# Layer-norm statistics of the second half by ScalarE, and a newer eviction as the marker of late input splits

## The chip, the cores and the metric

The kernel runs on one core of a Trainium2 chip. The metric is the device time of one execution in microseconds (us); lower is better. The engines are named as the profile names them: PE (TensorE, matmuls and transposes), DVE (VectorE), ACT (ScalarE), POOL (GpSimd) and SP (SyncE, which here only issues transfers).

## The reference

Two layers over 1024 tokens of width 1024: a gated linear recurrence (HGRN2), then a causal convolution module. Each is followed by a layer norm, a squared-ReLU MLP of width 4096, and another layer norm.

```python
for i in range(DEPTH):                       # DEPTH = 2
    mix = hgrn2_mixer(x, ...) if i % 2 == 0 else conformer_conv_mixer(x, ...)
    x = layer_norm(DEEPNORM_ALPHA * x + mix, ln_mix_g[i], ln_mix_b[i])
    ff = jnp.square(jax.nn.relu(x @ ffn_w1[i])) @ ffn_w2[i]
    x = layer_norm(DEEPNORM_ALPHA * x + ff, ln_ffn_g[i], ln_ffn_b[i])

def layer_norm(x, g, b):
    mu = jnp.mean(x, axis=-1, keepdims=True)
    var = jnp.mean(jnp.square(x - mu), axis=-1, keepdims=True)
    return (x - mu) * lax.rsqrt(var + LN_EPS) * g + b

# the end of hgrn2_mixer: o is (1024, 1024) after the recurrence and its own norm
return (o * silu(g)) @ w_out
```

All is in float32. The change concerns layer 0, where the recurrence's output is multiplied by `w_out` (the output projection), normed, and then multiplied by `ffn_w1[0]`.

## The kernel before

**Products.** A float32 product is made of three passes in the type fp32r. Each operand is split into a high part (a cast by ACT) and a low part (a subtraction by DVE, operand minus high part), and PE adds high times high, high times low and low times high. So an operand is ready for PE only after a cast by ACT and then a subtraction by DVE. The tensor with index 0 in its second dimension is the high part and with index 1 the low part.

**Forms.** The large products save multiplications as Strassen and Winograd do: two operands of 2 x 2 blocks are combined to seven forms each, and seven products take the place of eight. They run in the order `ORDER = (1, 2, 6, 5, 7, 3, 4)`. Forms 1 and 2 multiply single blocks; forms 6, 5 and 7 need sums or differences of blocks on both sides, form 3 on the side of the weights alone and form 4 on the side of x alone.

**The stages around the change.** The tokens fall into two halves of 512, each of four tiles t of 128. The output projection of half 0 comes first, then that of half 1. For each tile two products of 24 matmuls give 128 x 512 each; DVE adds the residual into `y[half][:, t]`, and `x1_block(half, t)` norms the tile and sends a copy to DRAM (`keep`). `norm` takes the statistics on DVE (two `bn_stats`, shown as BATCH_NORM_STATS2, and an aggregation), has POOL raise the variance to the power -1/2 (L518), and applies gain and offset in two DVE steps (SCALAR_TENSOR_TENSOR). `act_norm`, used elsewhere in the kernel, takes the sum and the sum of squares by two ACT passes with an accumulated output (L1083 and L1085 of the program before), writing the passed values into a tile `junk` that nobody reads.

The transposed halves are the blocks of x for the first MLP's up products (`Up`). PE transposes a normed tile against `ident` into a PSUM tile. From half 0 come forms 1 and 2 of x. From half 1 `x1_first(t)` makes form 5 and `x1_second(t)` form 6; they also leave unsplit values of forms 7, 3 and 4 in `late_x`. Those are split later by `x1_late(i, k)`: for i = 7, 3, 4 and each of the two pairs of 128-row blocks (k = 0 and k = 2) one cast of 128 x 1024 by ACT and one subtraction by DVE into `xf[i]`. These six calls are background chores; the first products of the MLP call them one after another. In the profile the tiles `xf[i]` are called x1f, `late_x` is xl (forms 7 and 3) and x (form 4), and all weights in use fw.

**The marker.** Ahead of each split `x1_late` has POOL copy one column into the tile that the split will write (L1191). Its value is overwritten at once; it is a marker, there so that the split is ordered behind whatever its source column depends on. Before, the source is the low part of the next weight in the queue.

**Weights of the first MLP.** `Up.form(c, i, f)` runs two products of 12 matmuls with form i of chunk c (eight chunks of 512 columns). The weights come as raw blocks by DMA. DVE adds blocks for the forms 6, 5, 7 and 3 of the first two chunks into tiles called `sum`, ACT casts them (L72), DVE subtracts (line 204, which is the line of every operation that DVE, PE and POOL's timed helper issue). `Up.form` evicts the PSUM of the opening forms into tiles called c by an ACT copy (L1266), for other forms adds PSUM into such a tile by DVE, and applies ReLU and the square by ACT (L1240 and L1241, `put`). The first products go in this order: forms 1 and 2 of chunk 0, forms 1 and 2 of chunk 1, then forms 6, 5, 7, 3, 4 of chunk 0, and the same of chunk 1.

**Sums in DRAM.** After all forms of chunk 0 the kernel calls `block_sums`, which prepares sums of blocks of the second MLP matrix in DRAM: a small transfer on SP's queue that waits for the last weight's low part (L418), two plain copies on SP's queue (L419, L420), and three transfers that POOL issues and that add to what is in DRAM (L421, L423, L423), each after the landing of the one before.

**What sets the order.** Up to `order.close()` (L1038), ahead of the output projection's second half, the order of instructions is written out by hand. Behind it a scheduler places the instructions of each engine by its own model of when operands are ready. The code's order is only its start, so a change in one dependence can move instructions of any engine. On the chip each engine then works through its list in order. The same holds for the DMA queues: a transfer that waits holds back those behind it on its queue.

**Memory.** The program places tiles by hand in 220 KB a partition with `view(kb, ...)`; a tile that is placed over another waits for the last use of that one.

Of the kernel before, what the change touches and what calls it, by code (L numbers as in the profile page):

```python
# [8 lines left out]
F32 = mybir.dt.float32  # L9
# [11 lines left out]
HT = 512  # L21
# [247 lines left out]
def body(ctx, tc, d, out):  # L269
    nc = tc.nc  # L270
# [9 lines left out]
    def view(kb, shape, dt=F32, name="t"):  # L280
        at, top = int(kb * 1024), KBYTES * 1024
        if at < edge[0]:
            if edge[0] < top:
                space.tile([P, (top - edge[0]) // 4], F32, name="gap")
            edge[0] = 0
        if at > edge[0]:
            space.tile([P, (at - edge[0]) // 4], F32, name="gap")
        edge[0] = at + (prod(shape) + 7) // 8 * 32
        return space.tile([P, *shape], dt, name=name)
# [788 lines left out]
    def act_norm(yt, g, b, junk, behind=None):  # L1078

        if behind is not None:  # L1080
            nc.gpsimd.tensor_copy(out=junk[:, :1], in_=behind)
        m = stat.tile([P, 5], F32, tag="mv", name="mv")
        nc.scalar.activation(junk, yt, AF.Copy, accum_out=m[:, 0:1])  # L1083
        vector.tensor_scalar(out=m[:, 1:2], in0=m[:, 0:1], scalar1=-1.0 / D, scalar2=None, op0=ALU.mult)
        nc.scalar.activation(junk, yt, AF.Square, bias=m[:, 1:2], accum_out=m[:, 2:3])  # L1085
        vector.tensor_scalar(out=m[:, 3:4], in0=m[:, 2:3], scalar1=1.0 / D, scalar2=LN_EPS, op0=ALU.mult, op1=ALU.add)
        power_m_half(m[:, 4:5], m[:, 3:4], 1)
        vector.scalar_tensor_tensor(out=yt, in0=yt, scalar=m[:, 1:2], in1=g, op0=ALU.add, op1=ALU.mult)
        vector.scalar_tensor_tensor(out=yt, in0=yt, scalar=m[:, 4:5], in1=b, op0=ALU.mult, op1=ALU.add)

    def norm(yt, g, b):
        mu, rs = moments(yt)
        vector.scalar_tensor_tensor(out=yt, in0=yt, scalar=mu, in1=g, op0=ALU.subtract, op1=ALU.mult)
        vector.scalar_tensor_tensor(out=yt, in0=yt, scalar=rs, in1=b, op0=ALU.mult, op1=ALU.add)
# [40 lines left out]
    g, b = gain(192, "ln_mix", 0)  # L1135
    y = [view(160 + 16 * h, (NTB, D), F32, "y") for h in range(2)][::-1]
    for half in range(2):
        for t in range(NTB):
            nc.sync.dma_start(out=y[half][:, t], in_=d["x"][half * HT + t * P : half * HT + (t + 1) * P])
    late_x = {4: view(212, (4, HT), F32, "x4")}  # L1140
    early = [Slots(nc, vector, slots((204,), "fw"), raws((0,))), Slots(nc, vector, slots((112, 120), "fw"), raws((96, 100)))]
    early.append(Slots(nc, vector, slots((144,), "fw"), raws((152,))))

    xf = {i: view(kb, (2, 4, HT), F32R, f"x1f{i}") for i, kb in ((6, 0), (5, 16), (3, 32), (1, 64), (2, 80), (7, 96), (4, 128))}
# [43 lines left out]
        less(x4, x4, of(xf[2], t, 1).bitcast(F32))  # L1188

    def x1_late(i, k):  # L1190
        nc.gpsimd.tensor_copy(out=xf[i][:, 0, k, :1], in_=fw.queue[0][:, 1, :1].bitcast(F32))  # L1191
        split(xf[i][:, 0, k : k + 2], xf[i][:, 1, k : k + 2], late_x[i][:, k : k + 2])

    def x1_block(half, t):
        norm(y[half][:, t, :], g, b)
        keep(half, t, y[half][:, t, :])
        if half == 0:
            bg.chores += [lambda k=k: turn(y[0][:, t, :], xf[1 + k // 4], t, k, 4) for k in (0, 4)]
            return
        if t == 0:  # L1200
            bg.done()
            late_x.update({i: view(kb, (4, HT), F32, "xl") for i, kb in ((7, 176), (3, 184))})
        if t < NTB - 1:
            bg.chores += [lambda: x1_first(t), lambda: x1_second(t)]
# [23 lines left out]
    class Up:  # L1228
# [23 lines left out]
        def form(self, c, i, f, copies=None, late=False):  # L1252

            u = self.of.setdefault(c, {})
            opens, turned = (1, 2, 3 if c == self.turned else 5), c == self.turned
            for q in range(2):
                parts = [(two(f, slice((q * 4 + k) * P, (q * 4 + k + 1) * P)), two(self.xf[i], k)) for k in range(4)]
                if i == 1:
                    u["z", q] = self.zs()
                if i in opens[1:]:  # L1260
                    u["w", q] = self.ws()
                ps = u["w" if i in (2, 5, 3) else "z", q]
                product(ps, parts, i in opens)
                if i in (1, 6, opens[2]):
                    t = u[i, q] = (copies or self.c)()
                    nc.scalar.copy(out=t, in_=ps)  # L1266
                elif i == 4:
                    self.put(u["h", q], 1, 0, self.c(), ps, -1.0)
                elif turned and i == 5:
                    t = u[6, q]  # L1270
                    vector.tensor_tensor(out=t, in0=t, in1=ps, op=ALU.add)
                    self.put(u["h", q], 0, 1, t, t, 1.0)
                    u[5, q] = u[3, q]
                    vector.tensor_tensor(out=u[5, q], in0=ps, in1=u[5, q], op=ALU.subtract)
                else:
                    t = u[{2: 1, 7: 5, 3: 6}[i], q]
                    vector.tensor_tensor(out=t, in0=t, in1=ps, op=ALU.add)
                    if i == 2:
                        if not late:
                            self.first(u, q)  # L1280
                        continue
                    m, n, scale = {7: (1, 1, -1.0), 3: (0, 1, 1.0)}[i]
                    self.put(u["h", q], m, n, t, t, scale)
            if i == 4:
                for q in range(2):
                    b = [[u["h", q][:, k, :, n * 256 : (n + 1) * 256] for n in range(2)] for k in range(2)]
                    t = {i: self.t() for i in (5, 6, 7, 4)}
                    forms_of(b, lambda i: t[i])
                    for i, src in ((1, b[0][0]), (2, b[1][0]), (3, b[1][1]), *t.items()):
                        store(self.layer, c, i, q, src)  # L1290
                del self.of[c]
# [164 lines left out]
    fw = Forms(nc, vector, slots((144, 152, 48, 112, 120), "fw"), raws(run(192, 4, 4)), raws(run(160, 2, 4), "sum"), lambda after: spare(after, True), 3, range(44))  # L1456
    fw.todo = [[(blocks("w1q", 0, c), 2 if c < 2 else 0)] for c in range(NFC)]
    up = Up()
# [25 lines left out]
    y = [view(32 + 16 * h, (NTB, D), F32, "y") for h in range(2)]  # L1484
    fw = Slots(nc, vector, slots([112, 120, 144, 152, 128, 136, 168], "dw"), raws([192, 196, 200, 204, 160, 164], "dr"), spare, 6, range(10, 50))
    fh = Slots(nc, vector, slots([0, 8, 16, 24, 96, 104, 176], "dh"))
    g, b = gain(184, "ln_ffn", 0)
# [300 lines left out]
    for op, i in steps:  # L1788
# [25 lines left out]
        elif op == "UB":  # L1814
# [5 lines left out]
            if i == NEAR - 1:  # L1820
# [5 lines left out]
                up = LateUp(xs)  # L1826
# [11 lines left out]
        else:  # L1838
# [4 lines left out]
            for k in LATER if i > NEAR else (3, 6, 5, 7, 4):  # L1843
# [3 lines left out]
                if i == NFC - 1 and k == 6:  # L1847
                    fw = Slots(nc, vector, slots([48, 104, 200, 208, 144, 152, 160], "dw"), raws([40, 176, 180, 44, 140, 136], "dr"))
# [7 lines left out]
    y = [view(kb, (NTB, D), F32, "y") for kb in (88, 112)]  # L1856
    g, b = gain(184, "ln_ffn", 1)
# [102 lines left out]
```

## Time and profile before

| | us |
|---|---|
| median of 3 runs | 2057.19 |
| lowest and highest run | 2056.47 and 2060.54 |
| the profiled execution's own time | 2057.16 |
| its span | 2055.4 |
| PE busy in it | 2023.6 |
| DVE busy | 1488.1 |
| ACT busy | 1094.5 |
| POOL busy | 396.3 |

The granted clock of PE averages 0.999 of full speed. The times in the prediction's rows count from the start of the span. In the timeline a row gives the start, the time from the first start to the last end, the engine, the line, the operation with its output and input, how many in a row (x), and in brackets for how long the engine had been idle and what it waited for last. In a row of the view by windows the columns are the window, its length, the busy time and number of instructions of PE, PE's weight loads, DVE, ACT and POOL, then PE's granted clock, the share of the DMA engines and what they moved in GB/s. The second half of the output projection runs from about 470 to 509 us, the MLP's products on forms 1 and 2 from there to 532, and forms 6, 5, 7, 3, 4 of chunk 0 from 532 on.

### The profile page before, as it was taken

The page shows a single profiled execution, that of the slowest core. Times are in us where ns is not written, and L with a number is a line of the kernel's source. Part 1 is how long each engine was busy: PE and PEld are TensorE (multiplying, and loading weights), DVE is VectorE, ACT ScalarE, POOL GpSimd, SP SyncE. Part 2 cuts the span into 40 slices and gives each one's busy share as a digit, 9 for nine tenths or more (in the row PEclk, how much of TensorE's full clock was granted, in tenths as well). Part 3 has the DMA queues.
Part 4 walks back from the last instruction along what each step waited for, and adds up shares of the span by engine and source line. Part 5 has one row for each costly group of instructions (what it writes and reads, how often), then busy time and mean ns, then how long its engine had stood idle before and what let it go on. Part 6 is the DMA issues. An engine that isn't in the chain of part 4 may idle for free. (4 is left out here: it accounts for less than half of the span.)

```text
span 2055.4 us, 29649 instructions
## 1 busy us (share of the span) xinstructions
PE 2023.6 (98%) x11144; PEld 1669.0 (81%) x11144; DVE 1488.1 (72%) x1978; ACT 1094.5 (53%) x1725; POOL 396.3 (19%) x405
## 2 busy tenths in 40 slices
PE   8999999999999999999999999999999999999998
PEld 7888887888787888888888888888888878888886
DVE  8698888877856675665567897889589666754456
ACT  5456565631655556444443776498615555443343
POOL 0112232111101000000001798089110000100002
PEclk9999999999999999999999999999999999999999
DMA  4778999842679776989998744496759768995542
GB/s 187 221 201 229 265 254 269 248 183 85 192 268 295 281 282 225 394 329 329 338 335 299 298 185 184 180 351 247 276 216 337 231 225 303 391 292 195 195 154 103
DMA packets 183944, 517.55 MB, mean 252 GB/s; under 512 B 17912, under 2 KB 49784, under 8 KB 182776
## 3 DMA queue, kind: packets, MB, share of 16 engines
q1 hardware_dynamic: 168312, 456.93, 61.7%
q0 software_dynamic: 15488, 58.72, 12.2%
q8 instruction: 87, 1.43, 0.3%
q14 instruction: 57, 0.47, 0.1%
HBM read 380.85 MB, written 201.85 MB: 283 GB/s over the span
## 5 line engine op out<-in xcount | busy, mean ns | idle before, releaser
L204 PE MATMUL ps<-dw,dh 128*128 128x512 f32 x2688 | 611.3, 389 | 0.5 <-DVE dh L204 0.5
L204 PEld LDWEIGHTS ps<-dw,dh 128*128 128x128 f32 x2688 | 504.3, 188 | 105.3 <-DVE dh L204 0.9
L204 PE MATMUL ps<-x1f,fw 128*128 128x512 f32 x1344 | 307.5, 390 | 5.2 <-ACT c L1266 2.3
L204 PEld LDWEIGHTS ps<-x1f,fw 128*128 128x128 f32 x1344 | 251.5, 188 | 59.7 <-issue 2.5
L204 PE MATMUL ps<-xf,fs 128*128 128x512 f32 x1008 | 248.6, 397 | 3.6 <-issue 1.7
L204 POOL TENSOR_TENSOR cb<-cb,prod 128x512 f32<-128x512 f32 x168 | 223.2, 1337 | 13.0 <-ACT prod L1591 2.4
L204 PEld LDWEIGHTS ps<-xf,fs 128*128 128x128 f32 x1008 | 184.0, 188 | 42.6 <-issue 1.9
L204 DVE TENSOR_TENSOR dh<-dh 128x1024 fp32r<-128x1024 f32 x112 | 136.5, 1222 | 109.4 <-ACT dh L72 109.3
L204 DVE SCALAR_TENSOR_TENSOR ps<-u,par,ps 128x512 f32<-128x512 f32 x296 | 206.0, 750 | 10.6 <-ACT ps L1603 9.3
L204 PE MATMUL ps<-xa,wa 128*128 128x512 f32 x864 | 203.3, 392 | 0.2
L72 ACT CAST dh<-dh 128x1024 fp32r<-128x1024 f32 x112 | 117.5, 1051 | 143.9 <-DMA dh<-hf 137.7
L72 ACT CAST dw<-dr 128x1024 fp32r<-128x1024 f32 x112 | 117.4, 1054 | 140.9 <-PE ps L204 125.5
L204 DVE TENSOR_TENSOR dw<-dr,dw 128x1024 fp32r<-128x1024 f32 x112 | 136.3, 1223 | 76.6 <-ACT dw L72 75.8
L204 PEld LDWEIGHTS ps<-xa,wa 128*128 128x128 f32 x864 | 160.3, 188 | 33.6 <-DMA wa<-ready 0.6
L1591 ACT ACTIVATE prod<-u,par 128x512 f32<-128x512 f32 x168 | 119.4, 726 | 34.2 <-POOL cb L204 33.5
L518 POOL TENSOR_TENSOR mv<-mv,nhalf 128x1 f32<-128x1 f32 x32 | 42.2, 1321 | 405.1 <-DVE mv L204 394.8
L204 PE MATMUL ps<-w,oT 128*128 128x512 f32 x384 | 89.9, 392 | 1.3 <-ACT oT L932 0.8
L204 PE MATMUL ps<-xb,wa 128*128 128x512 f32 x384 | 91.1, 393 | 0.0
L204 PE MATMUL ps<-vw,xf 128*128 128x512 f32 x336 | 79.9, 400 | 5.6 <-ACT vw L435 5.3
L204 PEld LDWEIGHTS ps<-w,oT 128*128 128x128 f32 x384 | 71.4, 188 | 16.6 <-ACT oT L932 1.2
L204 PEld LDWEIGHTS ps<-xb,wa 128*128 128x128 f32 x384 | 71.1, 188 | 14.3
L204 PEld LDWEIGHTS ps<-vw,xf 128*128 128x128 f32 x336 | 65.0, 194 | 20.1 <-ACT vw L435 5.3
(250 smaller groups left out, 2891.9 us busy)
## 6 DMA issues: line engine op xcount, KB each, us to landing
wa<-ready SPq DMA_DIRECT2D x140, 512.0 KB, 5.0
dh<-hf SPq DMA_DIRECT2D x112, 512.0 KB, 5.3
sum_w<-in_w_dram POOLq DMA_DIRECT2D x40, 1024.0 KB, 10.0
ready<-spare SPq DMA_DIRECT2D x76, 512.0 KB, 5.7
raw<-in_w1q_dram SPq DMA_DIRECT2D x66, 512.0 KB, 4.3
dr<-sum_w SPq DMA_DIRECT2D x64, 512.0 KB, 5.5
hf<-ht SPq DMA_DIRECT2D x112, 256.0 KB, 4.9
dr<-in_w_dram SPq DMA_DIRECT2D x48, 512.0 KB, 5.3
```

The source lines that it names most:

```text
L72: self.nc.scalar.copy(out=slot[:, 0, c], in_=raw[:, c])
L204: return op(*args, **kw)
L518: nc.gpsimd.tensor_tensor(out=dst, in0=src, in1=nhalf[:, :n], op=ALU.pow)
L1591: nc.scalar.activation(tp, u[:, k : k + HT], AF.Copy, scale=tap(j, k))
```

## The change

Two things change. In the second half of the output projection the statistics of the four tiles are taken by `act_norm`, and so by ACT, with a new junk tile of 4 KB at 200 KB. And the marker of `x1_late` copies a column of the newest tile that `Up.form` has evicted PSUM into, which is recorded as `up.mark`, in place of the next weight's low part.

```diff
-    late_x = {4: view(212, (4, HT), F32, "x4")}
+    junk, late_x = view(200, (1024,), F32, "junk"), {4: view(212, (4, HT), F32, "x4")}
...
     def x1_late(i, k):
-        nc.gpsimd.tensor_copy(out=xf[i][:, 0, k, :1], in_=fw.queue[0][:, 1, :1].bitcast(F32))
+        nc.gpsimd.tensor_copy(out=xf[i][:, 0, k, :1], in_=up.mark[:, :1])
         split(xf[i][:, 0, k : k + 2], xf[i][:, 1, k : k + 2], late_x[i][:, k : k + 2])

     def x1_block(half, t):
-        norm(y[half][:, t, :], g, b)
+        if half == 0:
+            norm(y[half][:, t, :], g, b)
+        else:
+            act_norm(y[half][:, t, :], g, b, junk)
         keep(half, t, y[half][:, t, :])
...
                 if i in (1, 6, opens[2]):
-                    t = u[i, q] = (copies or self.c)()
+                    t = u[i, q] = self.mark = (copies or self.c)()
                     nc.scalar.copy(out=t, in_=ps)
```

Lines move by up to three: L1240, L1241 and L1266 of the program before are L1243, L1244 and L1269 of the changed one. The lists below are those of the two programs; they say in which order an engine takes its instructions, not when.

First POOL, from the last power of the second half's norms to the third accumulating transfer. The tiles of x are called x1f with a number: before, 4510 is form 7, 4506 form 3 and 4512 form 4; in the changed program 4512 is form 7, 4508 form 3 and 4514 form 4. Before:

```order
L518 TENSOR_TENSOR mv<-mv,nhalf 128x1 x8
L1191 CAST x1f_4506<-fw 128x1 x2
L1191 CAST x1f_4510<-fw 128x1 x2
L421 DMA sum_w_5415<-in_w_dram 128x2x1024
L1191 CAST x1f_4512<-fw 128x1 x2
L423 DMA sum_w_5415<-sum_w_5415 128x1024 x2
```

The same stretch of POOL in the changed program, with c for an evicted tile:

```order
L518 TENSOR_TENSOR mv<-mv,nhalf 128x1 x8
L1191 CAST x1f_4512<-c_5144 128x1 x2
L1191 CAST x1f_4508<-c_5144 128x1
L421 DMA sum_w_5413<-in_w_dram 128x2x1024
L423 DMA sum_w_5413<-sum_w_5413 128x1024
L1191 CAST x1f_4514<-c 128x1
L423 DMA sum_w_5413<-sum_w_5413 128x1024
L1191 CAST x1f_4508<-c 128x1
L1191 CAST x1f_4514<-c 128x1
```

Before, all six markers stand ahead of both L423. In the changed program one for form 4 stands between them, and one each for forms 3 and 4 behind the second.

Next DVE, where the first sums of weight blocks for the forms 5 and 7 of chunk 0 are made. Before (c_5145 and c_5146 are the evicted tiles of form 1 that take the product on form 2; x1f_4504 is form 6, x1f_4509 form 2):

```order
L204 TENSOR_TENSOR xl<-xl,ps 128x4x128
L204 TENSOR_TENSOR x1f_4504<-y,x1f_4504 128x4x128
L204 TENSOR_TENSOR x_4488<-x_4488,x1f_4509 128x4x128
L204 TENSOR_TENSOR sum<-raw 128x1024
L204 TENSOR_TENSOR fw<-raw,fw 128x1024
L204 TENSOR_TENSOR c_5145<-c_5145,ps 128x512
L204 TENSOR_TENSOR sum<-sum,raw 128x1024
L204 TENSOR_TENSOR raw<-raw 128x1024
L204 TENSOR_TENSOR c_5146<-c_5146,ps 128x512
L204 TENSOR_TENSOR fw<-sum,fw 128x1024 x2
```

The same place of DVE in the changed program (c_5143 and c_5144 are those evicted tiles now, x1f_4506 is form 6):

```order
L204 TENSOR_TENSOR fw<-raw,fw 128x1024
L204 TENSOR_TENSOR xl<-xl,ps 128x4x128
L204 TENSOR_TENSOR c_5143<-c_5143,ps 128x512
L204 TENSOR_TENSOR x1f_4506<-y,x1f_4506 128x4x128
L204 TENSOR_TENSOR c_5144<-c_5144,ps 128x512
L204 TENSOR_TENSOR x1f_4512<-xl,x1f_4512 128x1024
L204 TENSOR_TENSOR sum<-raw 128x1024
L204 TENSOR_TENSOR x1f_4512<-xl,x1f_4512 128x1024
L204 TENSOR_TENSOR x1f_4508<-xl,x1f_4508 128x1024
L204 TENSOR_TENSOR sum<-sum,raw 128x1024
L204 TENSOR_TENSOR raw<-raw 128x1024
L204 TENSOR_TENSOR fw<-sum,fw 128x1024 x2
```

The first `sum` stood ahead of both additions into c; now it stands behind them and behind one low part of form 7 of x, with two more low parts of x ahead of the second `sum`.

Last ACT, at the late splits. Before, with L1045 for a cast of x, L72 for that of a weight and L1266 for an eviction:

```order
L72 CAST fw<-sum 128x1024
L72 CAST fw<-raw 128x1024
L1240 ACTIVATE c_5146<-c_5146 128x512
L1045 CAST x1f_4506<-xl 128x1024 x2
L1045 CAST x1f_4510<-xl 128x1024 x2
L1266 COPY c<-ps 128x512
L72 CAST fw<-sum 128x1024
L1045 CAST x1f_4512<-x_4488 128x1024 x2
```

The same casts in the changed program, from the first half of form 3 on:

```order
L1045 CAST x1f_4508<-xl 128x1024
L1243 ACTIVATE c_5144<-c_5144 128x512
L72 CAST fw<-sum 128x1024
L1244 ACTIVATE hr<-c 128x512
L72 CAST fw<-sum 128x1024
L72 CAST fw<-raw 128x1024
L72 CAST fw<-sum 128x1024
L1269 COPY c<-ps 128x512
L1045 CAST x1f_4514<-x_4490 128x1024
L72 CAST fw<-sum 128x1024
L1269 COPY c<-ps 128x512
L1045 CAST x1f_4508<-xl 128x1024
```

Before, the two casts of each late form stood together. Now the first cast of form 3 stands ahead of the first `sum`'s cast; its second stands behind the first cast of form 4, with weight casts and evictions between them.

## The prediction

> **What bounds the kernel now.** I read first the page's busy shares and the waits of PE, then PE's timeline around the change.
>
> ```profile
> PE 2023.6 (98%) x11144; PEld 1669.0 (81%) x11144; DVE 1488.1 (72%) x1978; ACT 1094.5 (53%) x1725; POOL 396.3 (19%) x405
> PE ps L204 <- ACT c L1266: 2.3, 2, 1.5
> PE ps L204 <- ACT fw L72: 1.5, 1, 1.5
> 524.24 8.21 PE L204 MATMUL ps<-x1f,fw 128*128 128x512 f32 x35
> 532.73 0.70 PE L204 MATMUL ps<-x1f,fw 128*128 128x512 f32 x2 [0.28 <-DVE c L204]
> 534.90 11.56 PE L204 MATMUL ps<-x1f,fw 128*128 128x512 f32 x48 [1.47 <-ACT fw L72]
> 547.94 72.36 PE L204 MATMUL ps<-x1f,fw 128*128 128x512 f32 x318 [1.47 <-ACT c L1266]
> ```
>
> PE is the bound, at 98%, so only what makes PE wait moves the time. From the second half of the output projection to the end of the first MLP's up products PE waits three times, 0.28 + 1.47 + 1.47 = 3.2 us: all between the last product on x forms 1 and 2 (ends 532.45) and the first on forms 3 and 7 (547.94). More than 3.2 us cannot be won here; that is 0.16% of 2057, less than the 0.2% that a measurement of this kernel can tell from no change. The undisturbed rate is 72.36 / 318 = 0.2275 us a matmul.
>
> **The statistics by ScalarE.** The last layer norm already uses `act_norm`, so its price is in the trace, beside the bn_stats path of the second half's first tile:
>
> ```profile
> 475.54 0.69 DVE L204 BATCH_NORM_STATS2 bs<-y 128x6 f32<-128x512 f32 x1
> 478.29 1.28 DVE L204 SCALAR_TENSOR_TENSOR y<-y,mv,ln_mix_b 128x1024 f32<-128x1024 f32 x1 [0.44 <-POOL mv L518]
> 2023.99 1.06 ACT L1083 ACTIVATE junk<-y 128x1024 f32<-128x1024 f32 x1 [4.37 <-DVE y L204]
> 2025.37 1.15 ACT L1085 ACTIVATE junk<-y,mv 128x1024 f32<-128x1024 f32 x1 [0.22 <-DVE mv L204]
> 2028.43 1.28 DVE L204 SCALAR_TENSOR_TENSOR y<-y,mv,ln_ffn_b 128x1024 f32<-128x1024 f32 x1 [0.44 <-POOL mv L518]
> ```
>
> From the start of the statistics to the last step of the norm: 2028.43 - 2023.99 = 4.44 us against 478.29 - 475.54 = 2.75, so a tile is ready 1.7 us later, and ACT works about 2.4 us more a tile. DVE saves two bn_stats and an aggregation a tile, about 1.4 us. I cost this at nothing for PE: the order puts the last tile's transposes 24 + 24 + 17 matmuls and eight transposes behind its last product (PE about 524.5, product done 509), and DVE's rows between them end the norm at about 519.6. The margin is 5 us; were it gone, each tile would cost up to 1.7 us. So PE reaches form 5 at 532.45 as before, with the same number of matmuls and transposes ahead.
>
> **The first form's weights come late.** Form 5 needs the cast of `sum` (three blocks of w1) by ACT. DVE's durations there:
>
> ```profile
> 524.52 0.69 DVE L204 TENSOR_TENSOR y<-x1f,ps 128x512 f32<-128x512 f32 x1 [2.24 <-PE ps L204]
> 529.63 1.22 DVE L204 TENSOR_TENSOR sum<-raw 128x1024 f32<-128x1024 f32 x1
> 530.76 1.22 DVE L204 TENSOR_TENSOR fw<-raw,fw 128x1024 fp32r<-128x1024 f32 x1
> 544.37 1.05 ACT L72 CAST fw<-sum 128x1024 fp32r<-128x1024 f32 x1
> 545.32 1.99 ACT L1045 CAST x1f<-x 128x1024 fp32r<-128x1024 f32 x2
> ```
>
> Row to row a 1024-wide DVE step takes 1.13 us (530.76 - 529.63), one of 512 about half that plus 0.03 (0.6), a 1024-wide cast by ACT 0.95 (545.32 - 544.37). In the changed order both adds into the tiles c_5143 and c_5144 and one low part of x form 7 stand ahead of `sum`. The add into c_5144 waits for the last product on form 2 (532.45, seen by DVE at 532.65). Then 0.6 + 1.13: `sum` starts at 534.4 and ends at 535.6, where it began at 529.63 before. ACT casts it by 537.0, behind a cast of x form 3 that a POOL mark releases at 534.4. PE waits 4.6 us. The next sum stands behind two more low parts (2 x 1.13), ends at 539.0, is cast at 540.05; the low part that PE needs then ends at 541.24. PE goes on at 541.3 with 40 of the 48 matmuls: 541.3 + 40 x 0.2275 = 550.4, 2.5 us behind the 547.94 of before.
>
> **The marks go behind the weight sums on POOL.** This is the large term.
>
> ```profile
> 532.39 0.32 SPq L418 DMA_DIRECT2D sum_w<-fw  x1
> 535.56 0.65 SPq L419 DMA_DIRECT2D sum_w<-in_w_dram  x1
> 536.72 3.68 POOL L1191 CAST x1f<-fw 128x1 fp32r<-128x1 f32 x4 [24.43 <-DVE fw L204]
> 542.03 1.27 POOL L421 DMA_DIRECT2D sum_w<-in_w_dram  x1 [1.63 <-DMA sum_w<-in_w_dram]
> 542.83 1.87 POOL L1191 CAST x1f<-fw 128x1 fp32r<-128x1 f32 x2
> 554.56 0.86 POOL L423 DMA_DIRECT2D sum_w<-sum_w  x1 [9.86 <-DMA sum_w<-in_w_dram]
> 563.02 0.81 POOL L423 DMA_DIRECT2D sum_w<-sum_w  x1 [7.59 <-DMA sum_w<-sum_w]
> ```
>
> POOL issues three accumulating transfers, each waiting on POOL for the landing of the one before. In the trace all six marks (L1191) are through before L423 waits. POOL works in order: the last two marks depended on a weight low part of about 538, yet ran only after L421's 1.63 us of waiting. Now the marks hang on evictions, and the order puts one mark for form 4 behind the first L423, and the last for forms 3 and 4 behind the second. ACT's casts that wait for them stand ahead of the weight cast and the evictions that PE needs next.
>
> Step by step. L418 waits for the low part of a weight that ended at 531.98; that DVE row now ends at 530.4 (525.15 for the first row above, 0.63 later as its transposes are later, then 0.72, 0.72, 0.67 for a cast, 0.6, 0.72, 0.6 and 1.22), 1.6 earlier. So L418 at 530.8; with the trace's own steps L419 + 3.17 = 534.0, L421 + 6.47 = 540.45, first L423 + 12.53 = 553.0, second L423 + 8.46 = 561.45. The first mark behind it is done 0.80 + 0.92 us on, at 554.7; ACT casts form 4 and then the weight (0.95 + 1.05), by 556.8. PE, there after six more matmuls at 551.8, waits 5.0 us, does 16 matmuls, and at 560.4 waits for form 3's second half: mark 561.45 + 0.80 + 0.92 = 563.2, cast + 1.1 = 564.3, low part + 1.25 = 565.55. In the trace this matmul, the 24th behind 547.94, starts at 547.94 + 23 x 0.2275 = 553.17. **Sum: 565.55 - 553.17 = 12.4 us later.** The 2.5 us above are inside it, as PE would wait here anyway, and what follows finds its operands ready. The profiled execution took 2057.16 (span 2055.4, 1.8 around it), the median is 2057.19, so they agree: **2069.5 us**.
>
> What is not certain is how long the transfers take to land. The trace's shortest and longest:
>
> ```profile
> 106.08 1.20 POOL L421 DMA_DIRECT2D sum_w<-in_w_dram  x1 [5.05 <-issue]
> 115.96 0.85 POOL L423 DMA_DIRECT2D sum_w<-sum_w  x1 [8.69 <-DMA sum_w<-in_w_dram]
> 122.80 0.87 POOL L423 DMA_DIRECT2D sum_w<-sum_w  x1 [4.55 <-DMA sum_w<-sum_w]
> 311.32 1.20 POOL L421 DMA_DIRECT2D sum_w<-in_w_dram  x1 [3.63 <-issue]
> 324.12 0.86 POOL L423 DMA_DIRECT2D sum_w<-sum_w  x1 [11.60 <-DMA sum_w<-in_w_dram]
> 634.68 0.85 POOL L423 DMA_DIRECT2D sum_w<-sum_w  x1 [7.50 <-DMA ready<-spare]
> 643.88 0.83 POOL L423 DMA_DIRECT2D sum_w<-sum_w  x1 [7.96 <-DMA hf<-ht]
> ```
>
> From L421 to L423 9.88 to 12.80, between the two L423 6.84 to 9.20; so 4.3 less or 1.0 more than taken, a loss of 8.1 to 13.4 us. I take this stage's own 12.53 and 8.46, since nearly the same loads of w1 run beside them.
>
> The Trainium skill, "DMA: Bandwidth & Descriptors", section "Anatomy of one DMA — SWDGE (gpsimd) path", fits such a transfer with about 2.0 us plus its bytes at 436 GB/s. By it, an estimate, the 1 MB transfer would take 4.4 us and the 0.5 MB one 3.2, the marks would come by 549.5, and only the late weights would be left. The trace disagrees: 12.53 and 8.46 us.
>
> **The rivals.**
> 1. The transfers land so early that no mark is late (L421 to L423 under 4.5 us). For it: the last mark is needed only at about 558. Against it: the trace's least is 9.88. Then only the 2.5 us remain: 2059.7. The skill's fit of the last paragraph gives this.
> 2. Not slower: DVE, relieved of 4 x 1.4 = 5.6 us, gets `sum` cast before PE reaches form 5, and the marks ahead of the transfers. It is decided on DVE at `sum`: if it ends before 531.4, the three waits go, 2057.16 - 3.2 = 2054.0. Against it: in the order, the add that waits for PE at 532.65 is ahead of `sum`.
> 3. PE restarts slowly after its long wait. The one long wait in the trace is at the start:
>
> ```profile
> 0.00:10.00 10.00, 4.74 (x11) 3.47 (x12) 3.28 (x5) 4.90 (x7) 0.80 (x8) 1.00 0.76 251
> 15.00:20.00 5.00, 5.00 (x24) 4.14 (x23) 4.44 (x6) 2.88 (x4) 0.00 (x0) 1.00 1.02 409
> ```
>
> After 5.26 us without work PE (first pair of numbers behind the comma) did 11 matmuls in 4.74 us, 0.43 each against 0.21 in the later row; at 0.2275 they take 2.5, so about 2.2 us are lost, with a granted clock of 1.00 (third from the end) all along. After the last wait here (3.9 + 1.0 us) the same would give 2069.5 + 2.2 = 2071.7; after the earlier ones it is hidden by the marks. For it: two waits of over 4.5 us now. Against it: the start may be slow for other reasons, as operands still arrive there. The Trainium skill, "TensorE: Matmul & The Clock Gate", Part 1, states that an idle window of about 3.4 us halves PE's clock until about as long of work; by that rule rival 3 comes true.
>
> **How the numbers follow.** Forecast (marks late, 2064.5 to 2071): 0.58. Rival 3, 2071.7: 0.22. Rival 1, 2059.7: 0.08. Rival 2, 2054.0: 0.06. A further wait that I have not seen, beyond 2074.5: 0.06. The range of 2063.0 to 2074.5 takes the first two with the bounds of the landings and 1.5 us of error in the walk at either end, and leaves out 0.20. Slower by over 0.2% (above 2061.3): 0.58 + 0.22 + 0.06 = 0.86. Within 0.2%: rival 1 and most of rival 2, 0.12; faster: 0.02.
>
> **What would show it.** In the changed profile: PE waits of 4 to 5 us at about 532 for ACT's cast of `fw`; POOL's L1191 standing behind both L423, whose waits for the landings now hold them; ACT idle for 8 us from about 546 and for 5 or so from 557 with POOL as releaser; two PE waits near 552 and 560. L1083 and L1085 four times between 475 and 513, with no PE wait before 532. It is wrong if the L423 waits are short, or if PE waits ahead of 532, where the norms' 5 us of margin would be mis-sized.

## The result, and the profile after

The changed kernel took 2065.87 us (median of 7 runs, 2062.47 to 2071.37), the kernel before 2058.52 (median of 7, 2056.47 to 2060.94). The ratio is 1.0033, with a 95% interval of 1.0018 to 1.0049: slower by 0.3%, some 7 us. The forecast was 2069.5 in a range of 2063.0 to 2074.5.

First the page of the changed kernel (busy times) and the rows of its view of waits that bear on the stage: what PE waited for between 470 and 700 us (in all, times, longest):

```profile
PE 2028.1 (98%) x11144; PEld 1672.0 (81%) x11144; DVE 1482.5 (72%) x1970; ACT 1101.0 (53%) x1741; POOL 395.4 (19%) x405
PE ps L204 <- ACT fw L72: 6.8, 3, 4.6
PE ps L204 <- DVE x1f L204: 0.8, 1, 0.8
```

The profiled execution of the change took 2068.57, that of before 2057.16. Not all of these 11.4 us are the change's. The output projection starts at 416.30 here and at 411.54 in the profile of before, and up to there the code is the same. In the profiles below that start lies anywhere from 413 to 421. So I measure from the stage's own start: from the first matmul on x1f (509.00 before, 513.33 now) to the end of the 432nd, well behind the late splits. Before, the trace has that end at 613.04, so 104.0 us. Now, from PE's timeline:

```profile
513.33 1.07 PE L204 MATMUL ps<-x1f,fw 128*128 128x512 f32 x4
529.75 7.29 PE L204 MATMUL ps<-x1f,fw 128*128 128x512 f32 x31
541.61 2.08 PE L204 MATMUL ps<-x1f,fw 128*128 128x512 f32 x4 [4.57 <-ACT fw L72]
544.70 13.98 PE L204 MATMUL ps<-x1f,fw 128*128 128x512 f32 x50 [1.01 <-ACT fw L72]
559.85 4.22 PE L204 MATMUL ps<-x1f,fw 128*128 128x512 f32 x17 [1.17 <-ACT fw L72]
564.84 98.44 PE L204 MATMUL ps<-x1f,fw 128*128 128x512 f32 x433 [0.76 <-DVE x1f L204]
```

The last row begins with the 168th matmul, and the 432nd ends at 625.20, which is 111.9 us from the start: +7.9. Up to 537.04 there is no wait, so the norms by ScalarE were hidden. Then come the two kinds of wait that the forecast named: 4.57 us for the first weight's cast, and two near 560 and 564. What stands out is how short the last two are. DVE's timeline shows why the first weight is late:

```profile
537.15 0.69 DVE L204 TENSOR_TENSOR c<-c,ps 128x512 f32<-128x512 f32 x1 [0.47 <-PE ps L204]
537.75 1.22 DVE L204 TENSOR_TENSOR x1f<-xl,x1f 128x1024 fp32r<-128x1024 f32 x1
538.89 1.22 DVE L204 TENSOR_TENSOR sum<-raw 128x1024 f32<-128x1024 f32 x1
```

The first sum is behind an addition that itself waits for PE, and behind a low part of form 7. POOL's timeline, with the markers (L1191) and the accumulating transfers:

```profile
532.29 0.77 POOL L1191 CAST x1f<-c 128x1 fp32r<-128x1 f32 x2 [11.80 <-ACT c L1269]
537.90 1.11 POOL L1191 CAST x1f<-c 128x1 fp32r<-128x1 f32 x1 [4.84 <-DVE c L204]
542.66 1.27 POOL L421 DMA_DIRECT2D sum_w<-in_w_dram  x1 [3.64 <-DMA sum_w<-in_w_dram]
555.74 0.86 POOL L423 DMA_DIRECT2D sum_w<-sum_w  x1 [11.81 <-DMA sum_w<-in_w_dram]
556.29 1.48 POOL L1191 CAST x1f<-c 128x1 fp32r<-128x1 f32 x1
561.44 0.81 POOL L423 DMA_DIRECT2D sum_w<-sum_w  x1 [3.68 <-DMA sum_w<-sum_w]
561.98 0.47 POOL L1191 CAST x1f<-c 128x1 fp32r<-128x1 f32 x1
```

POOL waits 11.81 us for the landing ahead of the first L423 and 3.68 for that ahead of the second, and a marker stands behind each. ACT's timeline shows what they hold:

```profile
550.61 0.59 ACT L1269 COPY c<-ps 128x512 f32<-128x512 f32 x1 [0.34 <-PE ps L204]
557.80 1.05 ACT L1045 CAST x1f<-x 128x1024 fp32r<-128x1024 f32 x1 [6.60 <-POOL x1f L1191]
558.76 1.04 ACT L72 CAST fw<-sum 128x1024 fp32r<-128x1024 f32 x1
562.47 1.05 ACT L1045 CAST x1f<-xl 128x1024 fp32r<-128x1024 f32 x1 [2.20 <-POOL x1f L1191]
```

The tile that the first of these markers reads is evicted by 551.2; the marker runs at 556.29, 5 us later. ACT stands idle for 6.60 us for it, then casts form 4 of x, and only then the weight that PE waits for at 559.85. And the clock, by windows (third figure from the end):

```profile
530.00:539.00 9.00, 7.04 (x31) 5.47 (x30) 8.35 (x13) 6.17 (x9) 1.87 (x3) 1.00 0.17 32
540.00:549.00 9.00, 6.38 (x14) 4.59 (x15) 9.00 (x9) 4.18 (x6) 1.27 (x1) 0.50 1.02 279
550.00:559.00 9.00, 8.68 (x39) 6.86 (x37) 2.57 (x3) 2.06 (x4) 2.03 (x2) 1.00 0.77 228
```

Behind the wait of 4.57 us PE runs at half its clock: 14 matmuls in 6.38 us busy, 0.46 each. So PE came late to the markers by itself. Whether the 7.9 us belong to the markers, to the late weights or to the clock cannot be read from this profile alone, since they overlap.

### The profile page after: what moved, and what is told of

It is laid out like the page before. It is cut to its first block, busy times and chain, and to the rows that moved or that the text cites. A ratio compares the mean times of both kernels' runs of the same rounds, so it can differ in the third digit from the quotient of the medians.

```text
span 2066.8 us, 29668 instructions
## 1 busy us (share of the span) xinstructions
PE 2028.1 (98%) x11144; PEld 1672.0 (81%) x11144; DVE 1482.5 (72%) x1970; ACT 1101.0 (53%) x1741; POOL 395.4 (19%) x405
## 3 DMA queue, kind: packets, MB, share of 16 engines
q0 software_dynamic: 15488, 58.72, 12.4%
## 4 chain that ended last, share of the span: by engine, by line
PE 66%; DMA 17%; DVE 7%; issue 5%; ACT 3%; POOL 2%; SPq 0%; DVEq 0%; POOLq 0%; ACTq 0%
PE ps L204 66%; DMA sum_w<-in_w_dram 7%; DMA raw<-in_w1q_dram 1%; POOL cb L204 1%; DMA dr<-in_w_dram 1%; DMA sum_w<-sum_w 1%; DMA next<-in_w1q_dram 1%; DMA next<-in_w_dram 1%; DMA hf<-ht 1%; DVE spare L204 1%; DMA vr<-in_wv_dram 1%; DVE qk L204 1%; DVE fw L204 1%; ACT spare L1448 1%; DVE y L204 1%
## 5 line engine op out<-in xcount | busy, mean ns | idle before, releaser
L204 DVE SCALAR_TENSOR_TENSOR ps<-u,par,ps 128x512 f32<-128x512 f32 x296 | 206.2, 750 | 10.9 <-ACT ps L1606 9.4
L72 ACT CAST dh<-dh 128x1024 fp32r<-128x1024 f32 x112 | 117.4, 1051 | 155.7 <-DMA dh<-hf 155.4
L72 ACT CAST dw<-dr 128x1024 fp32r<-128x1024 f32 x112 | 117.2, 1052 | 128.5 <-PE ps L204 108.9
L1243 ACT ACTIVATE c<-c 128x512 f32<-128x512 f32 x72 | 44.8, 628 | 70.4 <-DVE c L204 70.0
```

The costliest lines, as they stand in the source:

```text
L72: self.nc.scalar.copy(out=slot[:, 0, c], in_=raw[:, c])
L204: return op(*args, **kw)
L1243: nc.scalar.activation(t, src, AF.Relu, scale=scale)
```

## The experiments

Theory M, the forecast's: the markers behind POOL's transfers set the end, and the late weights lie inside. Theory A: the late weights and the half clock behind the long wait set it, and the markers are covered. All results first; "first 432" is the measure above, "waits" PE's waits in it, "half clock" the time in it at a granted clock of 0.50. "Stage" runs from the same start to the first matmul on dw and dh, where the next products begin; the expectations for norm_alone, mark_alone, sums_later and fill_later go by this one. The other expectations quote the first 432 as read from merged rows, within 0.2 us of the table. Each ratio is to runs of before beside it on the same chip, whose medians were 2058.1 to 2060.5.

| kernel | median us | ratio to before (95%) | first 432 | waits | half clock | stage |
|---|---|---|---|---|---|---|
| before | 2058.52 |  | 104.0 | 3.2 | none | 313.2 |
| before_again | 2057.48 (1 run) |  | 104.0 | 3.2 | none | 313.1 |
| the change | 2065.87 | 1.0033 (1.0018 to 1.0049) | 111.9 | 7.5 | 10.2 | 321.1 |
| after_again | 2069.80 | 1.0037 (1.0024 to 1.0050) | 110.7 | 6.5 | 10.2 | 319.6 |
| norm_alone | 2059.04 | 0.9991 (0.9979 to 1.0002) | 106.0 | 3.0 | 6.8 | 312.9 |
| mark_alone | 2064.55 | 1.0023 (1.0008 to 1.0039) | 110.2 | 5.8 | 6.8 | 318.4 |
| sums_later | 2071.89 | 1.0057 (1.0038 to 1.0076) | 109.7 | 5.6 | 10.2 | 324.1 |
| fill_later | 2068.07 | 1.0037 (1.0022 to 1.0053) | 108.5 | 1.9 | 3.4 | 320.7 |
| mark_act | 2063.22 | 1.0022 (1.0012 to 1.0032) | 107.8 | 4.7 | 6.8 | 317.8 |
| last_bn_markact | 2059.05 | 1.0005 (0.9990 to 1.0020) | 105.2 | 3.0 | 3.4 | 312.7 |
| last_bn_old | 2057.97 | 0.9995 (0.9983 to 1.0008) | 104.2 | 3.4 | none | 314.3 |
| bn_markact | 2061.89 | 0.9999 (0.9990 to 1.0009) | 106.3 | 3.4 | 6.8 | 313.7 |
| norm_fill | 2059.32 | 1.0012 (0.9997 to 1.0027) | 104.6 | 0.5 | none | 312.5 |
| mark_act_fill | 2064.62 | 1.0027 (1.0011 to 1.0042) | 107.2 | 2.3 | none | 316.6 |

The two measures can differ, since PE waits again between 655 and 676 us, for 1.9 us before, not at all in norm_alone and 2.8 in mark_act. Differences of the first 432 under 0.4 us say nothing: in the kernels that norm the third tile by ScalarE four more transposes fall into that stretch.

### Each edit alone

norm_alone takes the marker back to the weight's low part; mark_alone takes the norms back.

```diff
 norm_alone:
-        nc.gpsimd.tensor_copy(out=xf[i][:, 0, k, :1], in_=up.mark[:, :1])
+        nc.gpsimd.tensor_copy(out=xf[i][:, 0, k, :1], in_=fw.queue[0][:, 1, :1].bitcast(F32))
 mark_alone:
-        if half == 0:
-            norm(y[half][:, t, :], g, b)
-        else:
-            act_norm(y[half][:, t, :], g, b, junk)
+        norm(y[half][:, t, :], g, b)
```

> The statistics by ScalarE alone; the marker copies the next weight's low part again, as before. Measure: from the first matmul on x1f to the first on dw,dh, 313.18 us before and 321.11 with the change (+7.93). On POOL all six markers stand ahead of both L423. On DVE the first sum stays behind both additions into c, but the low part of form 7 of x no longer stands ahead of it. Theory A (PE waits for late weights, and runs at half its clock behind a long wait): the wait for the first sum's cast is about 4.57 - 1.13 = 3.4 us, one more of 0.5, less the 3.2 us of before, and some 2 us of half clock: +2.7, and the clock shows under 0.9 after the wait. Theory B (the clock has no part): +0.7. Theory C (all of the loss hangs on the markers behind L423): 0 or less.

> The newer marker alone; statistics by bn_stats for all tiles, as before. On DVE the first sum stands ahead of the additions into c again; on POOL one marker of form 3 stands behind the first L423 and one of form 4 behind the second, and PE's list now has twelve matmuls of form 3 in a row, whose second half needs that marker. Measure as above. Theory A, markers behind L423: L418 at 23.4 us from the first matmul on x1f, L421 at 33.0, first L423 at 45.6 to 46.1, low part of form 3 at 49.4; PE is there at 38.8 and waits 10.6 us, then runs at half clock for 3 to 4 us: +11 (9 to 13). Without any part of the clock: +9. Theory C', only late weights matter and markers are covered: -1.5 to +0.5.

norm_alone came to +2.0 in the first 432, with one PE wait:

```profile
544.41 286.39 PE L204 MATMUL ps<-x1f,fw 128*128 128x512 f32 x1248 [2.99 <-ACT fw L72]
```

That is close to A's +2.7, with the half clock behind the wait. But the expectation named the whole stage, and there norm_alone is at -0.3, as C had it: no PE wait of later chunks is left, where before had two more (0.85 and 1.08 us), and the whole kernel is no slower than before. mark_alone came to +6.2 in the first 432 and +5.2 over the stage, less than the +11 that I expected with the markers behind L423, and far from C'. Its POOL, and PE at the markers:

```profile
549.60 0.75 POOL L1191 CAST x1f<-c 128x1 fp32r<-128x1 f32 x1 [2.39 <-ACT c L1266]
558.22 0.86 POOL L423 DMA_DIRECT2D sum_w<-sum_w  x1 [7.87 <-DMA sum_w<-in_w_dram]
558.77 0.51 POOL L1191 CAST x1f<-c 128x1 fp32r<-128x1 f32 x1
```

```profile
541.09 18.23 PE L204 MATMUL ps<-x1f,fw 128*128 128x512 f32 x66 [0.41 <-DVE c L204]
560.41 0.50 PE L204 MATMUL ps<-x1f,fw 128*128 128x512 f32 x1 [1.08 <-ACT x1f L1045]
```

L423 was where I put it (558.22 - 512.30 = 45.9 us from the start; 45.6 to 46.1 expected). But PE needed the second half of form 3 later than I had read from the list: it did 66 matmuls without it, some of them at half the clock. Most of the loss sits with the marker edit: +6.2 against +2.0 in the first 432, +5.2 against -0.3 over the stage.

### The markers taken off POOL's queue

sums_later calls `block_sums` after chunk 1 in place of chunk 0; mark_act leaves it and copies the marker on ACT; bn_markact does the same to mark_alone.

```diff
 sums_later:
-        if c in (0, 2):
+        if c in (1, 2):
             block_sums(*to_sum.pop(0), f[:2, 1, :1].bitcast(F32))
 mark_act, and bn_markact with norm() for all tiles:
-        nc.gpsimd.tensor_copy(out=xf[i][:, 0, k, :1], in_=up.mark[:, :1])
+        nc.scalar.copy(out=xf[i][:, 0, k, :1], in_=up.mark[:, :1])
```

> The change, but block_sums is called after chunk 1 in place of chunk 0, so all six markers stand ahead of L421 on POOL; DVE's list around the first sum is that of the change. Theory A (late weights and the half clock behind them set the end, the markers' wait lies inside it): waits of 4.57 + 1.01 stay, 3.2 of before go, and about 3.7 us are lost at half clock: +6. Theory M (the markers set the end, as forecast; the late weights by themselves are worth 2.5 us): +2.4. Waits near L1191 must be gone in both.

> The change, with the markers copied by ACT in place of POOL, so that no marker stands behind an accumulating transfer and the sums in DRAM stay where they were; DVE's first sum stays behind the additions into c. Measure: the first 432 matmuls on x1f, which took 104.0 us before, 111.8 with the change, 109.7 in sums_later. Theory A (the late weights and the half clock behind the long wait are worth about 5.7, the markers some 2 on top): 109.5, with a PE wait of 4.5 us, half clock behind it, and no wait for L1045 or x1f near the 150th matmul. Theory M (the markers set the end): 106.4.

> mark_alone with the markers copied by ACT: bn_stats for all tiles, the newer marker, no marker on POOL. If the queue behind L423 is what mark_alone pays for (the first 432 matmuls took 110.3 us): 105.0, as last_bn_markact, so -5.3; the wait at the first sums stays at 1.3 to 2.6. If the marker's newer source costs by itself, by the order it makes on ACT and DVE: 109 or more.

sums_later's first 432 were +5.7, close to A's +6; over the stage, which the expectation named, it is +10.9, which neither theory had. Its waits:

```profile
539.06 2.08 PE L204 MATMUL ps<-x1f,fw 128*128 128x512 f32 x4 [4.57 <-ACT fw L72]
542.14 78.29 PE L204 MATMUL ps<-x1f,fw 128*128 128x512 f32 x332 [1.01 <-ACT fw L72]
625.31 89.45 PE L204 MATMUL ps<-x1f,fw 128*128 128x512 f32 x384 [4.87 <-ACT c L1269]
```

The first two are the change's own, and those at the markers are gone. The whole is slower than the change, by a wait that no kernel with the sums in their old place has (4.87 us; 2.61 in fill_later, which moves the sums too). I did not follow it up. It begins at 620.4, where the first 432 have just ended, so it spoils the stage and the whole time but not the first 432. Markers aside, the traces of sums_later and of the change show the same order of work on PE, and for the first 100 us of the stage on DVE and ACT. So sums_later tells what the wait of the markers alone is worth: 109.7 against 111.9 and 110.7, or 1.0 to 2.2 us, as much as PE's last waits in the change's two profiles (1.9 and 1.0).

mark_act came to 107.8, between A's 109.5 and M's 106.4. Its PE still waits 4.25 us for the late weight, and no more for markers:

```profile
538.82 2.08 PE L204 MATMUL ps<-x1f,fw 128*128 128x512 f32 x4 [4.25 <-ACT fw L72]
541.10 2.07 PE L204 MATMUL ps<-x1f,fw 128*128 128x512 f32 x4 [0.20 <-ACT fw L72]
543.38 118.80 PE L204 MATMUL ps<-x1f,fw 128*128 128x512 f32 x520 [0.20 <-DVE fw L204]
```

Against the mean of the change's two profiles, 111.3, that is -3.5 us with the late weights kept. But this edit moves more than the markers: on DVE a late split of x goes behind the second sum, so that the second weight is waited for 0.20 us in place of 1.01, and the half clock lasts 6.8 us in place of 10.2. bn_markact against mark_alone gives 110.2 - 106.3 = 3.9 without the late norms (5.3 expected), again with a sum and an activation in other places; its 106.3 lies between the 105.0 and the 109 that were expected. So waiting behind L423 is worth 1.0 to 2.2 us by itself, and 3.5 to 3.9 with the order that comes with a marker on ACT. Neither theory was right alone, and A was the nearer on what the markers are worth.

### What makes the weights late

```diff
 last_bn_markact (mark_act's marker) and last_bn_old (the marker of before):
-        if half == 0:
+        if half == 0 or t == NTB - 1:
             norm(y[half][:, t, :], g, b)
```

> As mark_act, with the last tile's statistics by bn_stats again (three tiles by ScalarE). In the lists this alone brings the first sum back ahead of the additions into c, but two casts of form 7 of x stand ahead of the first sum's cast on ACT. If the last tile's longer norm is what made the weights late: the PE wait at the first sum falls from 4.57 to 2.0 or less, the first 432 matmuls take 107.6 with a half clock behind that wait (6.8 us of it in mark_alone, whose wait was 2.61) and 105.5 without. If the weights are late for another reason: 109.5, as mark_act.

> Three tiles' statistics by ScalarE, the last by bn_stats, the marker as before. DVE's and ACT's lists at the first sums are nearly those of before. If the statistics by ScalarE are free wherever the last tile is left out: 104.0 within 0.7 for the first 432 matmuls, no PE wait over 1.5 us, no half clock, time as before. If ACT's extra 2.4 us a tile cost PE something of their own: over 105.5.

With bn_stats for the last tile alone, the first sum goes ahead of the addition again (DVE of last_bn_markact), and the long PE wait splits into two short ones:

```profile
530.36 1.22 DVE L204 TENSOR_TENSOR sum<-raw 128x1024 f32<-128x1024 f32 x1
531.50 1.22 DVE L204 TENSOR_TENSOR fw<-raw,fw 128x1024 fp32r<-128x1024 f32 x1
532.63 0.68 DVE L204 TENSOR_TENSOR c<-c,ps 128x512 f32<-128x512 f32 x1
```

```profile
535.63 1.19 PE L204 MATMUL ps<-x1f,fw 128*128 128x512 f32 x4 [1.29 <-ACT fw L72]
538.50 125.75 PE L204 MATMUL ps<-x1f,fw 128*128 128x512 f32 x546 [1.68 <-DVE c L204]
```

From mark_act's 107.8 this is -2.6 us, to 105.2 (105.5 was expected without a half clock, 107.6 with one; 3.4 us of it came). That is the price of the last tile's longer norm with the newer marker; with the old marker it is 1.8 (norm_alone against last_bn_old). PE pays it by the order on DVE. last_bn_old came out at 104.2 and 0.9995, as expected: ACT's statistics for the other three tiles are free, and win nothing. It had one wait over the expected 1.5 (2.11 us at 551.83).

### What the half clock costs

The fill kernels put matmuls that nobody reads into the place of PE's long wait: 20 in fill_later (on sums_later), 13 in norm_fill (on norm_alone), 18 in mark_act_fill (on mark_act).

```diff
+    for _ in range(18):
+        tensor.matmul(banks[:, 3], xf[6][:, 1, 3, :P], xf[6][:, 1, 3], start=True, stop=True)
     up.settle(0)
     fw.ahead(3)
```

> As sums_later, with twenty more matmuls (128x512, high by low part of form 6 of x, into a PSUM bank that nobody reads) between form 2 of chunk 1 and the first form behind it, so that PE is busy while it would have waited 4.57 us. DVE's list is that of sums_later. If the wait is what halves the clock: granted clock 1.00 throughout, +2.4 us against before, 3.7 less than sums_later. If the clock falls for another reason (heat, a transfer), or its fall costs nothing: as sums_later.

> norm_alone with thirteen more matmuls (as in fill_later; nobody reads them) in the place of its PE wait of 2.99 us. The lists of the other engines are the same up to the forms 3 and 7. Granted clock 1.00 there if the wait is what halves it. If the half clock of 6.8 us costs PE what it takes: the first 432 matmuls 3.0 us shorter than norm_alone's 106.0, so 103.0, and the time 3 us below before's. If ACT's casts and DVE's low parts of x are due at that time anyway: PE waits about 1.0 for the first low part and 1.8 for the weight of form 3, and 105.3.

> mark_act with eighteen more matmuls (nobody reads them) in the place of its PE wait of 4.25 us; the lists of all other engines are the same throughout. Granted clock 1.00 in place of 6.8 us at half. If the half clock costs what PE loses by it (some 5.8 us of work at half, 2.9 us): 104.7 for the first 432 matmuls against 107.6. If the weights' casts and low parts, 1.0 us apart each, are waited for in its place: 106.7.

mark_act_fill is the cleanest: apart from the fill, PE, DVE and ACT work in mark_act's order all through the first 432. The clock, mark_act and then mark_act_fill:

```profile
538.00:544.60 6.60, 5.37 (x11) 3.37 (x12) 6.60 (x7) 3.49 (x4) 1.26 (x1) 0.50 1.03 299
```

```profile
540.00:551.00 11.00, 8.69 (x36) 6.20 (x35) 10.52 (x12) 7.88 (x11) 1.26 (x1) 1.00 0.85 264
```

So the wait is what halves the clock: fill it, and the clock stays at 1.00. Yet the first 432 hardly moved, 107.8 to 107.2, and the ratio of the whole did not fall (1.0022 and 1.0027). PE of mark_act_fill:

```profile
545.23 1.19 PE L204 MATMUL ps<-x1f,fw 128*128 128x512 f32 x4 [0.15 <-ACT fw L72]
547.50 1.19 PE L204 MATMUL ps<-x1f,fw 128*128 128x512 f32 x4 [1.08 <-ACT fw L72]
549.78 118.58 PE L204 MATMUL ps<-x1f,fw 128*128 128x512 f32 x520 [1.08 <-DVE fw L204]
```

The 5.37 us of work at half clock cost mark_act 2.7 us, but with the full clock PE waits 1.08 us for the second weight's cast and 1.08 for its low part, where mark_act had 0.20 each: the weights come no faster. norm_fill says the same (104.6 against norm_alone's 106.0, so 1.4 of the 3.0 that were expected if the half clock cost what it takes; 1.0012 against 0.9991 for the whole). fill_later is weaker evidence: 1.2 us were won (108.5 against 109.7; 3.5 over the stage, where the second wait shrank too), and its clock was not at 1.00 throughout, as a wait of 1.87 us still brought 3.4 us at half clock. So of A's half clock some 0.6 to 1.4 us are left; most of its cost is time that PE would have waited for operands anyway.

### The same kernels again

> The kernel before, unchanged, for a second profile: how far the first 432 matmuls on x1f (104.0 us) and the transfers' landings repeat. If one profile is a fair measure: 104.0 within 0.7, no half clock in this stage. The 8.46 us between the two L423 is 5.6 to 6.5 in every other profile so far; if it belongs to the kernel before it repeats, if it was chance it comes out near 6.

> The change, unchanged, for a second profile: 111.8 within 1.0 for the first 432 matmuls, PE waits of about 4.6 and 1.0 at the first sums, then one or two waits behind L423, half clock for about 10 us. The start of the output projection (416.3 us in the first profile, 411.5 in that of before, 413 to 421 in the experiments, with the same lists up to there) should differ again, by chance alone.

The measure repeats to 0.1 us for before and to 1.2 for the change, which is more than the 1.0 that I expected; the waits and the half clock came as expected. The output projection started at 414.3 in before_again and 414.8 in after_again, so the 4.8 us between the first two profiles ahead of the stage were chance. The time between the two L423 was 7.70 in before_again and 5.73 in after_again, so the long one does belong to the kernel before, which the next section takes up.

## Why the prediction was right, and where it was not

The direction, the range and the two mechanisms held; the size of the main term did not, nor how far the marks bind. By its own steps:

- **What PE waits for before: misread.** The forecast counted three waits to the end of the up products, 3.2 us. Its own row says 2.3 us in two waits for ACT's eviction, of which it took one; the trace has five waits, 5.2 us, the last two of 0.85 and 1.08 us at 657 and 664. So 5.2 us could be won, not 3.2. The forecast time does not hang on it, but norm_alone's -0.3 over the stage does.
- **The statistics at nothing: right.** PE has no wait ahead of 537.04; the last tile's norm ended 4.8 us ahead of its transposes (5 were forecast), and three tiles by ScalarE give 104.2 (last_bn_old). What the forecast did not say is that the last tile's statistics are also what puts the weight sum behind the additions, its next step.
- **The first form's weights late: right in place and size.** 4.6 us were forecast for PE's wait at the end of form 2, and 4.57 came. PE was then to end its 48 matmuls 41.4 us from the stage's start. It ended them at 44.4 in the change and at 42.4 with the clock kept (mark_act_fill), so by that comparison 1.0 us was mis-sized and 2.0 were the clock.
- **The marks go behind the weight sums: right as a mechanism, mis-sized.** The forecast put the matmul that waits last at 56.6 us from the start of the stage, 12.4 later than before. It came at 564.84 - 513.33 = 51.5; the same matmul, the 168th, stood at 43.8 before (the forecast took the 170th), so it came 7.7 later, which is nearly all of the +7.9. Of the 5.0 us between 56.6 and 51.5, 2.1 were won by L421 (29.3 us from the start, 31.4 forecast, since L419 followed L418 by 1.12 us in place of 3.17), 0.6 lost at the first L423 (13.08 us behind L421 against 12.53), 2.8 won at the second (5.70 against 8.46), and 0.7 won from there to the matmul.
- **The step that failed** is the choice of these landings: "since nearly the same loads of w1 run beside them". For the second transfer that was not so. In the profile of before, SP's queue issues two loads of w1 (L135) and the first stores of the MLP's results (hf, L1226 there) while it lands, and the DMA engines are 92% busy (second figure from the end in the windows); in the change SP issues nothing in that time, and the 5.70 us lie below every landing that the prediction had found in the trace (6.84 the least).

Before, SP's queue and the window from the first to the second L423:

```profile
558.56 0.33 SPq L135 DMA_DIRECT2D raw<-in_w1q_dram  x1
559.14 0.38 SPq L1226 DMA_DIRECT2D hf<-hr  x1
559.70 0.47 SPq L135 DMA_DIRECT2D raw<-in_w1q_dram  x1
562.60 1.50 SPq L1226 DMA_DIRECT2D hf<-hr  x3
```

```profile
555.00:563.00 8.00, 8.00 (x37) 6.62 (x36) 7.07 (x9) 6.45 (x10) 0.42 (x1) 1.00 0.92 212
```

The change, the same (SP from 553 us on):

```profile
562.40 11.51 SPq L135 DMA_DIRECT2D raw<-in_w1q_dram  x3
574.42 0.38 SPq L1229 DMA_DIRECT2D hf<-hr  x1
```

```profile
555.70:561.40 5.70, 4.53 (x21) 3.42 (x20) 3.74 (x4) 2.48 (x3) 2.03 (x2) 1.00 0.56 109
```

The delay that I forecast emptied the queue that I had taken the price from. In last_bn_old, where three loads start between the two L423 (558.34 and 564.84) but the first store only at 564.49, the time between them is 6.50, against 8.46 and 7.70 in the two profiles of before. That the neighbours lengthen the landing is read from these traces, not from an experiment that moves loads or stores alone.

- **How far the marks bind: mis-sized too.** The forecast had the late weights, 2.5 us, inside the marks' 12.4, so that early marks would have won 9.9. The marks did come last in the change, but sums_later, without their wait, is still at +5.7: they bind by 1.0 to 2.2 us. PE was late by itself, from the late weights, the newer marker's order and the half clock, which the forecast left unpriced as hidden.
- **The range held with some luck.** The loss was 7.35 us (2065.87 - 2058.52), less than the 8.1 that the shortest landings gave, or 2065.3. The time still lies above that bound, because before itself took 1.3 us more here than the 2057.19 that the forecast was added to.
- **Rival 1** (no mark late) is out: ACT waits 6.60 us for one. The fit of the Trainium skill beside it, "DMA: Bandwidth & Descriptors", section "Anatomy of one DMA — SWDGE (gpsimd) path", made the landings 4.4 and 3.2 us; the profile has 13.08 and 5.70.
- **Rival 2** (not slower) is out: the sum stood behind the addition, as the order had it.
- **Rival 3** (PE restarts slowly) happened, at another place than the one where I gave it a price: behind the first long wait, for 10.2 us, and not behind the last. Its 2.2 us on top did not come: the last waits were 1.17 and 0.76 us, and the clock behind them was 1.00. The rule of the Trainium skill, "TensorE: Matmul & The Clock Gate", Part 1, has the clock halved by an idle window of about 3.4 us; the trace agrees with the halving (0.50 behind the wait of 4.57 us). The cost was mostly hidden, as the forecast said of the earlier waits: in the change the marks came later still, and in mark_act the weights. The forecast misread its own row for this rival: the trace of before has no record of the clock ahead of 11.6 us, and the view prints 1.00 there. Up to that moment a matmul took 0.427 us and behind it 0.227, the same two rates as at 0.50 and 1.00 in the change, so that the slow start was most likely half clock too.

What the edits cost depends on what else is changed. In the first 432 the wait of the markers on POOL is worth 1.0 to 2.2 us with the other lists kept, the last tile's longer norm 1.8 to 2.6, and the newer marker's order on ACT and DVE 1.0 to 2.3 (last_bn_markact against last_bn_old, bn_markact against before). Over the whole stage the parts do not add up at all: the norms alone give -0.3 (norm_alone), the newer marker with its copy on ACT +0.5 (bn_markact), and both together +4.6 (mark_act); the whole times go the same way, 0.9991, 0.9999 and 1.0022. The newer marker on POOL without the norms gives +5.2 (mark_alone), and all of it 7.9 and 6.4. So the norms and the newer marker cost little by themselves, and the norms' late weights or POOL's queue, added to the newer marker, each bring most of the loss. Why they combine so was not taken apart further. No version here beats the kernel before by more than a measurement can tell; last_bn_old (0.9995), bn_markact (0.9999) and norm_alone (0.9991) are level with it.

## What to carry to other kernels

A marker is an instruction on some engine's list: before hanging it on something newer, see what else waits in that list. Here a one-column copy was ready 5 us before the queue ahead of it let it run; putting it on the engine that acts on it took 3.5 us off the first 432, though not the rest of the loss. And a wait that ends last need not be worth its length: without it the next path may end almost as late, as sums_later shows. A duration taken from a trace holds only while its neighbours stay where they are: where the change itself moves the neighbours, price the landing from the emptier stretches too. A slow clock behind a wait is a symptom until the wait is filled and the time is seen to fall.

## What the runs showed of the hardware that was not expected

The half clock comes in whole steps: each stretch of it inside a profile lasts 3.4, 6.8 or 10.2 us, but for the last, which the end of the kernel cuts off. It takes less than a long wait: in last_bn_markact waits of 1.29 and 1.68 us close together brought 3.4 us of it, and 2.99 in norm_alone brought 6.8. But it is not a matter of length alone, since 2.11 us in last_bn_old (at 552), 2.61 in fill_later (at 622) and even 3.46 in after_again (from 266 on, in the recurrence) brought none.
